# A decoder trunk whose eight experts take their places in another order

## The chip, the cores and the metric

The kernel runs on one core of one Trainium2 chip. The metric is the time of one execution on the device, in microseconds (us). One further execution was taken by the hardware profiler; its rows are what the prediction argues from. Of the core's engines four matter here: TensorE (matmuls; PE in the rows, and PEld for its weight loads), VectorE (DVE), ScalarE (ACT), and SyncE (SP), which computes nothing and issues the loads from memory (DMAs).

## The reference

The model has two layers over 256 tokens of width 1024, all in 32-bit floats. Each layer has a token mixer (attention) and a channel mixer, each followed by a layer norm, and ends with a small gated embedding term. The first layer's channel mixer is dense. The second's is a mixture of eight experts of hidden width 3584, of which every token uses two:

```python
logits = (x @ w_router).astype(jnp.float32)
top_v, top_i = lax.top_k(logits, TOP_K)          # TOP_K = 2 of 8
top_w = jax.nn.softmax(top_v, axis=-1)
gates = jnp.sum(jax.nn.one_hot(top_i, N_EXPERTS) * top_w[..., None], axis=-2)
for e in range(N_EXPERTS):
    out = out + gates[..., e:e + 1] * swiglu(x, w_gate[e], w_up[e], w_down[e])
```

Here `swiglu` is `(silu(x @ w_gate) * (x @ w_up)) @ w_down`. The three matrices of one expert hold 3 x 1024 x 3584 numbers.

## The kernel before

The kernel runs the first layer, the second layer's attention, and then the function `moe`, in which the change lies. There the router picks two experts for every token and counts how many tokens each expert has. The eight experts are then worked through in eight *places*, one after the other. A place doesn't hold a fixed expert: `RANKS` (line 53) says for each place which expert it takes, by its rank in the order of counts. Expert 0 always has rank 0 and the first place; of the others a lower rank has more tokens. The function `order` (lines 721 to 753) turns this into the list `ordi` of expert numbers by place, and SP reads an expert's number from it before the loads of that place (`block_of`, line 973), so that the loads go to that expert's weights.

A place is built for a fixed number of tokens, called slots. Ranks of 5 and above (`SMALL`, line 52) are the three experts with the fewest tokens, and their places have `CS` = 64 slots; the other five have `CM` = 96. Line 925 makes the list:

```python
small = [r >= SMALL for r in RANKS]
groups = [(CS if v else CM) // CG for v in small]
```

Slots are gathered, multiplied and scattered in groups of 32 (`CG`), so a place of 96 slots, called medium here, has three groups and one of 64, called small, has two. A group of 32 token columns is loaded into a quarter of TensorE's array and the weights stream past it (`gate_up_quads` at line 895, `down_quads` at 882 and 885, and the loop at 1141 for the down matmuls of a small place). So a block of weights costs TensorE less in a small place, while the bytes that it takes to load are the same. If an expert has more tokens than slots, extra passes under `tc.If` do the rest; they are outside the order of places.

Within a place the hidden width is cut into four chunks (`CHUNKS`, line 51) of 4, 8, 8 and 8 blocks of 128. The list `seq` (lines 961 to 971) writes the whole work out by hand, block by block: for each chunk the gate-and-up blocks (`w`), then the down blocks (`d`) of the chunk before. Thus the last chunk's down blocks of one place come after the first chunk of the next, and the first chunk of a place is also the end of a stretch that begins in the place before. Gathering the tokens of the next place and scattering the sums of the last one are hung between blocks (`next_expert`, `scatter`). TensorE, VectorE, ScalarE and GpSimd keep this order.

Loads run ahead of the work. `take` issues the loads for as many blocks as the ring of buffers has, and each goes out on SP's queue when its buffer is free, in the order of `seq`. The ring has 21 buffers of 1 MB at first, 20 from the 27th block on, and for the last 26 blocks eight, since the rest are needed by the ending. A block is a gate half and an up half of 512 KB each (issued at line 994), or one down block of 1 MB (line 121). The first chunk of the first place is loaded and multiplied ahead of this list, for all tokens.

After the last place the function `ending` adds the last expert's sums, and does the layer norm and the gated embedding term.

Of the kernel before, what the change touches and what calls it, by code (L numbers as in the profile page):

```python
# [49 lines left out]

CHUNKS = [(0, 4), (4, 8), (12, 8), (20, 8)]
SMALL = 5
RANKS = [0, 5, 1, 2, 6, 3, 7, 4]

# [7 lines left out]
def trunk(ctx: ExitStack, tc: tile.TileContext, a: dict, out: bass.AP):  # L64
# [598 lines left out]
    def route(i, xT, rp, wrh, wrl):  # L663
# [5 lines left out]
        def small(n=NE):  # L669
            at = [next(cells) for _ in range(n // 2)][0]  # L670
            return sm[:, at:at + n]
# [43 lines left out]
        prank = small()  # L715
        for n, r in enumerate(RANKS):
            nc.gpsimd.memset(prank[:, n:n + 1], float(r))
# [54 lines left out]
    def moe(i, x, xT, router, pj):  # L772
        j = i // 2
        with tc.tile_pool(name=f"route{i}", bufs=1, reuse_waits="tile") as rp:
# [49 lines left out]
            def slots(e, p1, small):  # L824

                pe = []
                for t in range(NT):
                    q = rp.tile([P, C], F32, tag=f"pe{t}", bufs=1, name=f"pe{t}")
                    o, v = q, iota1
                    if small:  # L830
                        o = q.rearrange("p (a s) -> p a s", a=2)
                        v = iota1[:, None, :CS].to_broadcast([P, 2, CS])
                    nc.vector.tensor_scalar(o, v, p1[t][:, e:e + 1], None, op0=ALU.is_equal)
                    pe.append(q)
                return pe
# [86 lines left out]
            def main_experts(p1, name, first):  # L922


                small = [r >= SMALL for r in RANKS]
                pe, peT, ob, hT = slots(0, p1, False), None, None, {}
# [627 lines left out]
```

## Time and profile before

| | |
|---|---|
| median of 3 runs | 1344.87 us (1344.11 to 1345.36) |
| the profiled execution | 1344.83 us |
| its span, from the first instruction to the last | 1343.0 us |
| TensorE matmuls, busy | 1311.2 us, 98% of the span |
| bytes read from memory | 433.63 MB |
| mean granted clock of TensorE | 0.995 of full speed |

TensorE counts as busy nearly all the time. Matmuls are pipelined and their ends are modelled, so a share near 100% says that matmuls were in flight and not that the engine was at its peak. The loads of the expert weights share the stretch from about 480 us on with the matmuls that use them.

### The profile page before, as it was taken

What the parts mean: (1) busy time and instruction counts of PE and PEld (TensorE: products, weight loads), DVE (VectorE), ACT (ScalarE), POOL (GpSimd) and SP (SyncE); (2) the same over time, 40 slices, a digit from 0 to 9 for tenths busy, and PEclk for the clock granted to TensorE, in tenths of its full rate; (3) what the DMA queues carried; (4) which work ended last, traced back from release to release, by engine and by line L of the source; (5) the groups of instructions that cost most, each with busy time, mean ns of one, the idle gap of its engine ahead of it and who ended that gap; (6) DMA issues with size and microseconds to landing.
All of it is one profiled execution on the core that took longest, in us unless ns stands there. A gap on an engine that the chain in (4) does not pass through costs nothing.

```text
span 1343.0 us, 29864 instructions
## 1 busy us (share of the span) xinstructions
PE 1311.2 (98%) x12815; PEld 764.9 (57%) x12815; DVE 431.7 (32%) x843; ACT 319.0 (24%) x609; POOL 12.9 (1%) x38
## 2 busy tenths in 40 slices
PE   8999999999999999999999999999999999799987
PEld 6778888888787743453544443363543453343346
DVE  7777444445778611011020011012011011011036
ACT  6865444444458300010000000000000000001013
POOL 1000000000000000000000000000000000000000
PEclk9999999999999999999999999999999999999999
DMA  8439555535358699999999999999999999999970
GB/s 327 156 122 311 190 188 188 188 126 188 119 178 293 262 375 367 402 376 418 414 418 418 415 418 418 415 413 415 414 413 417 409 417 418 408 416 416 415 313 35
DMA packets 141356, 436.71 MB, mean 325 GB/s; under 512 B 11808, under 2 KB 12576, under 8 KB 141216
## 3 DMA queue, kind: packets, MB, share of 16 engines
q1 hardware_dynamic: 141216, 434.72, 83.1%
q8 instruction: 103, 1.69, 0.5%
q14 instruction: 37, 0.30, 0.1%
HBM read 433.63 MB, written 1.05 MB: 324 GB/s over the span
## 4 chain that ended last, share of the span: by engine, by line
PE 82%; DMA 13%; DVE 3%; ACT 1%; issue 1%; POOL 0%; DVEq 0%; SPq 0%; POOLq 0%; ACTq 0%
PE we L895 30%; PE eoe L882 11%; DMA raw_we<-in_w_exp_up_dram 10%; PE eoe L1141 4%; DMA raw_de<-in_w_exp_down_dram 3%; PE gf L159 2%; PE gf L160 2%; PE uf L160 2%; PE uf L159 2%; PE gf L161 2%; PE uf L161 2%; PE fo L159 2%; PE fo L160 2%; PE fo L161 2%; PE pg L936 2%; PE qkv L160 2%
## 5 line engine op out<-in xcount | busy, mean ns | idle before, releaser
L895 PE MATMUL we<-raw_we,xs_e 128*32 128x512 f32 (+1 forms) x5184 | 508.6, 545 | 6.4 <-DMA raw_we<-in_w_exp_up_dram 6.4
L895 PEld LDWEIGHTS we<-raw_we,xs_e 128*32 128x32 f32 x5184 | 166.5, 110 | 318.6 <-issue 280.5
L1033 DVE TENSOR_TENSOR sgh<-we,sgh 128x256 f32<-128x256 f32 (+1 forms) x81 | 32.0, 395 | 590.4 <-ACT sgh L1030 588.8
L882 PE MATMUL eoe<-raw_de,hT 128*32 128x256 f32 x2520 | 186.5, 379 | 0.0
L885 PE MATMUL eoe<-raw_de,hT 128*32 128x256 f32 x840 | 185.3, 379 | 0.0
L1030 ACT ACTIVATE sgh<-we 128x256 f32<-128x256 f32 (+1 forms) x81 | 29.1, 360 | 563.1 <-PE we L895 563.1
L882 PEld LDWEIGHTS eoe<-raw_de,hT 128*32 128x32 f32 x2520 | 103.6, 110 | 77.8 <-issue 5.4
L885 PEld LDWEIGHTS eoe<-raw_de,hT 128*32 128x32 f32 x840 | 92.0, 110 | 0.0
L1141 PE MATMUL eoe<-raw_de,hT 128*32 128x256 f32 x1344 | 77.0, 380 | 4.7 <-DMA raw_de<-in_w_exp_down_dram 4.7
L1141 PEld LDWEIGHTS eoe<-raw_de,hT 128*32 128x32 f32 x1344 | 42.7, 110 | 38.7 <-DMA raw_de<-in_w_exp_down_dram 6.1
L159 PE MATMUL fo<-hi_df,hTh 128*128 128x512 f32 x112 | 43.7, 390 | 0.8 <-ACT hTh L164 0.8
L143 DVE TENSOR_TENSOR lo_gf<-raw_gf,hi_gf 128x1024 fp32r<-128x1024 f32 x28 | 33.2, 1222 | 34.9 <-ACT hi_gf L139 34.9
L143 DVE TENSOR_TENSOR lo_df<-raw_df,hi_df 128x1024 fp32r<-128x1024 f32 x28 | 33.5, 1221 | 33.8 <-ACT hi_df L139 33.8
L159 PE MATMUL gf<-hi_gf,xT_b 128*128 128x512 f32 x112 | 44.2, 394 | 0.0
L161 PE MATMUL gf<-hi_gf,xT_b 128*128 128x512 f32 x112 | 43.7, 390 | 0.0
L161 PE MATMUL uf<-hi_uf,xT_b 128*128 128x512 f32 x112 | 43.7, 390 | 0.0
L159 PE MATMUL uf<-hi_uf,xT_b 128*128 128x512 f32 x112 | 43.7, 390 | 0.0
L160 PE MATMUL gf<-lo_gf,xT_b 128*128 128x512 f32 x112 | 43.6, 389 | 0.0
L160 PE MATMUL fo<-lo_df,hTh 128*128 128x512 f32 x112 | 43.6, 389 | 0.0
L160 PE MATMUL uf<-lo_uf,xT_b 128*128 128x512 f32 x112 | 43.6, 389 | 0.0
L161 PE MATMUL fo<-hi_df,hTl 128*128 128x512 f32 x112 | 43.3, 389 | 0.0
L143 DVE TENSOR_TENSOR lo_uf<-raw_uf,hi_uf 128x1024 fp32r<-128x1024 f32 x28 | 33.1, 1219 | 19.1 <-ACT hi_uf L139 19.1
(292 smaller groups left out, 1596.7 us busy)
## 6 DMA issues: line engine op xcount, KB each, us to landing
raw_de<-in_w_exp_down_dram SPq DMA_DIRECT2D x111, 1024.0 KB, 12.4
raw_we<-in_w_exp_gate_dram SPq DMA_DIRECT2D x220, 512.0 KB, 10.1
raw_we<-in_w_exp_up_dram SPq DMA_DIRECT2D x220, 512.0 KB, 10.0
raw_uf<-in_w_ffn_up_dram SPq DMA_DIRECT2D x14, 1024.0 KB, 5.0
raw_gf<-in_w_ffn_gate_dram SPq DMA_DIRECT2D x14, 1024.0 KB, 5.0
raw_df<-in_w_ffn_down_dram SPq DMA_DIRECT2D x14, 1024.0 KB, 4.7
raw_qkv<-in_w_qkv_dram SPq DMA_DIRECT2D x11, 1024.0 KB, 5.9
raw_wo<-in_w_o_dram SPq DMA_DIRECT2D x8, 1024.0 KB, 5.6
```

What stands on the lines that cost most here:

```text
L143: nc.vector.tensor_tensor(lo[:, cs], raw[:, cs], hi[:, cs].bitcast(F32), op=ALU.subtract)
L159: nc.tensor.matmul(o, xh, wh, start=start, stop=False)
L160: nc.tensor.matmul(o, xh, wl, start=False, stop=False)
L161: nc.tensor.matmul(o, xl, wh, start=False, stop=stop)
L882: nc.tensor.matmul(b[q * CG:(q + 1) * CG, c:c + CQ], xh(q), w[:, k, c0:c0 + CQ], start=start, stop=stop)
L885: nc.tensor.matmul(b[3 * CG:, c:c + CQ], xh(r), w[:, k, c0:c0 + CQ], start=start, stop=stop)
L895: nc.tensor.matmul(b[qs, :2 * nb * CG].rearrange("p (m b r) -> p m b r", m=2, b=nb), xe[:, k, g * CG:(g + 1) * CG], w[..., qs], start=firs ...
L936: nc.tensor.matmul(pg[:, k * n:(k + 1) * n], x[t][:, (h * nk + k) * P:(h * nk + k + 1) * P], pe[t][:, :n], start=t == 0, stop=t == NT - 1)
L1030: nc.scalar.activation(sg[:, g * cols:(g + 1) * cols], b[:, :cols], AF.Silu)
L1033: nc.vector.tensor_tensor(h, b[:, cols:2 * cols], h, op=ALU.mult)
L1141: nc.tensor.matmul(ob[0][q * CG:(q + 1) * CG, r * CQ:(r + 1) * CQ], hT[e, f][:, g, k, :], half[:, k % 2, c * CB + r * CQ:c * CB + (r + 1) ...
```

## The change

One line: the list of ranks by place. The small places, those with a rank of 5, 6 or 7, are the second, third and sixth after the change, and the second, fifth and seventh before it. The medium places come in the same order among themselves, and so do the small ones.

```diff
 CHUNKS = [(0, 4), (4, 8), (12, 8), (20, 8)]
 SMALL = 5
-RANKS = [0, 5, 1, 2, 6, 3, 7, 4]
+RANKS = [0, 5, 6, 1, 2, 7, 3, 4]
```

## Rows read from the trace of the kernel before

**Rows 1.** The page: span, TensorE's busy time, GB/s of loads in forty slices.

```profile
span 1343.0 us, 29864 instructions
PE 1311.2 (98%) x12815; PEld 764.9 (57%) x12815; DVE 431.7 (32%) x843; ACT 319.0 (24%) x609; POOL 12.9 (1%) x38
GB/s 327 156 122 311 190 188 188 188 126 188 119 178 293 262 375 367 402 376 418 414 418 418 415 418 418 415 413 415 414 413 417 409 417 418 408 416 416 415 313 35
```

**Rows 2.** The page's DMA issues: tile, queue, count, size, us to landing.

```profile
raw_de<-in_w_exp_down_dram SPq DMA_DIRECT2D x111, 1024.0 KB, 12.4
raw_we<-in_w_exp_gate_dram SPq DMA_DIRECT2D x220, 512.0 KB, 10.1
```

**Rows 3.** Timeline of TensorE: start, length; second chunk's first matmuls, places 2 to 8.

```profile
595.45 1.90 PE L895 MATMUL we<-raw_we,xs_e 128*32 128x512 f32 x16
...
678.40 3.19 PE L895 MATMUL we<-raw_we,xs_e 128*32 128x512 f32 x28
...
794.03 3.19 PE L895 MATMUL we<-raw_we,xs_e 128*32 128x512 f32 x28
...
905.89 1.47 PE L895 MATMUL we<-raw_we,xs_e 128*32 128x512 f32 x12
...
988.84 2.74 PE L895 MATMUL we<-raw_we,xs_e 128*32 128x512 f32 x22
...
1100.70 3.62 PE L895 MATMUL we<-raw_we,xs_e 128*32 128x512 f32 x32
...
1198.42 1.92 PE L895 MATMUL we<-raw_we,xs_e 128*32 128x512 f32 x16 [0.90 <-DMA raw_we<-in_w_exp_up_dram]
```

**Rows 4.** Timeline of SP: the issue of the same block's gate half, places 3 to 8.

```profile
646.75 0.81 SPq L994 DMA_DIRECT2D raw_we<-in_w_exp_gate_dram  x1
...
754.08 0.34 SPq L994 DMA_DIRECT2D raw_we<-in_w_exp_gate_dram  x1
...
860.96 0.54 SPq L994 DMA_DIRECT2D raw_we<-in_w_exp_gate_dram  x1
...
967.58 0.69 SPq L994 DMA_DIRECT2D raw_we<-in_w_exp_gate_dram  x1
...
1074.97 0.82 SPq L994 DMA_DIRECT2D raw_we<-in_w_exp_gate_dram  x1
...
1181.46 0.40 SPq L994 DMA_DIRECT2D raw_we<-in_w_exp_gate_dram  x1
```

**Rows 5.** Waits of TensorE, 1110 to 1200 us: total, times, longest.

```profile
PE we L895 <- DMA raw_we<-in_w_exp_up_dram: 6.4, 11, 0.9
PE eoe L1141 <- DMA raw_de<-in_w_exp_down_dram: 4.7, 7, 1.5
```

**Rows 6.** Waits of SP, 652 to 1074 us.

```profile
SPq L994 <- DMA raw_de<-in_w_exp_down_dram: 82.1, 45, 3.2
...
SPq L121 <- DMA raw_we<-in_w_exp_up_dram: 17.0, 28, 0.8
SPq L994 <- PE we L895: 7.7, 13, 1.5
...
SPq L994 <- PE eoe L1141: 0.3, 1, 0.3
```

**Rows 7.** Stretches: length, busy time of each engine, clock, DMA share, GB/s.

```profile
652.00:1074.00 422.00, 422.00 (x5355) 188.82 (x5355) 49.07 (x96) 26.09 (x67) 0.00 (x0) 1.00 1.03 415
...
800.00:820.00 20.00, 20.00 (x207) 7.05 (x209) 6.68 (x12) 2.66 (x7) 0.00 (x0) 1.00 1.03 420
...
1140.00:1160.00 20.00, 14.58 (x167) 4.75 (x156) 0.00 (x0) 0.00 (x0) 0.00 (x0) 1.00 1.02 403
...
1300.00:1320.00 20.00, 14.12 (x51) 10.43 (x51) 17.93 (x33) 10.26 (x20) 1.47 (x2) 0.74 0.11 41
```

**Rows 8.** Timelines of SP and TensorE: last expert loads issued, last down matmuls.

```profile
1279.06 0.89 SPq L121 DMA_DIRECT2D raw_de<-in_w_exp_down_dram  x2
...
1299.32 0.39 PE L882 MATMUL eoe<-raw_de,hT 128*32 128x256 f32 x3
```

## The prediction

> **What bounds the kernel now.** I read the page first. It shows TensorE busy for 98% of the span and the loads near 415 GB/s from the nineteenth of its forty slices to the thirty-eighth [rows 1], so it does not say which of the two sets the end. The listing of DMA issues comes next: the expert weights come in 1 MB blocks, either one down block or a gate and an up half of 512 KB [rows 2]. A place takes 28 gate-and-up blocks and 14 down blocks, 42 in all, whether its expert has 96 slots or 64: 44.04 MB. Only TensorE's work depends on the slots.
>
> So I set up two clocks, both read at the same block of every place, the first of its second chunk. From the timeline of TensorE I take when it starts that block, M2 to M8 for places 2 to 8 [rows 3]. From the timeline of SP I take when that block's load is issued, I3 to I8 [rows 4].
>
> - TensorE's steps. M2 to M3 82.95 us (a small place, then a medium one), M3 to M4 115.63 (medium, medium), M4 to M5 111.86 (medium, small), M5 to M6 82.95 (small, medium), M6 to M7 111.86, M7 to M8 97.72. The last is again small to medium, and should have been 82.95: there TensorE stood 14.77 us.
> - The stream's steps. 107.33, 106.88, 106.62, 107.39, 106.49 us; the mean is 106.94 (534.71 / 5), whatever TensorE does.
>
> That is the whole picture: TensorE takes longer than the stream over a medium place (111.86 or 115.63 against 106.94), and about 24 us less over a small one. What it has in hand is M minus I, less the least that this can be. The block at M8 was started the moment its load came (its row names the DMA as releaser), so the least is 1198.42 - 1181.46 = 16.96 us. Spare at M3 to M8 is then 14.7, 23.0, 28.0, 4.3, 8.8 and 0 us. The waits of TensorE stand where this ledger puts them: the view of waits shows it waiting for loads between 1110 and 1200 us, some half a microsecond a block, 6.4 and 4.7 us in its rows [rows 5]. (They sum to less than 14.77; the ends of matmuls in the trace are modelled, so the starts are the safer reading.) From M8 on it works without a wait to the last down matmul at 1299.3 us, and then comes the ending, whose matmuls and vector work are the same in both kernels [rows 8].
>
> **The change, part by part.** Removed and added instructions: none. The two lists hold the same five medium and three small places, so the matmuls, gathers, scatters and loads are the same in number, and so are the bytes. `RANKS` also fills the small table `prank`, with eight one-element writes whatever the numbers are. The register loads on SP that find an expert's weights stay one a place, at the same blocks. What moves is which place is small: 2, 3, 6 in place of 2, 5, 7. I price it by running the ledger again with the same steps.
>
> - Up to the start of place 3 nothing differs.
> - M3. The step is now small to small, which the trace does not have. Replacing the next place by a small one took 115.63 - 111.86 = 3.77 us off a step (the four blocks of the next place's first chunk that lie in it, and its gather), so it is 79.18. Between 79.18 and the 82.95 of the nearest row the end does not change, since a wait follows. Spare at M3: 14.69 - 3.77 = 10.9.
> - M4, small to medium: 82.95 - 106.94 = -24.0. Spare would be -13.1: TensorE waits 13.1 us in place 3 and is at 0.
> - M5, medium to medium: +8.7. M6, medium to small: +4.9, so 13.6.
> - M7, small to medium: -24.0, so -10.4: TensorE waits 10.4 us in place 6 and is at 0.
> - M8, medium to medium: +8.7. TensorE starts the block 16.96 + 8.69 us after its issue: 1181.46 + 25.65 = 1207.11, where it was 1198.42.
>
> The sum is 8.7 us. Waits say the same: 13.1 + 10.4 = 23.5 us against 14.8. In words: before, the last wait lay in place 7 and one medium place was left after it. Now it lies in place 6 and two are left, and over a medium place that follows another TensorE needs 8.7 us more than the stream. The spare time that the loads had gained over places 3 and 4 before (28.0 us at its height) is no longer there to be used up, because small places 2 and 3 in a row empty it at once.
>
> What follows M8 I cost at nothing. Place 8 is the same work, and the loads are further ahead by 8.7 us. For the last loads the ring shrinks to eight blocks, so some of them will be issued up to 8.7 us later, when TensorE has freed the block; the last one went out at 1279.06 and its last matmuls ran at 1299.32, 20 us later [rows 8], and a delay equal to TensorE's own leaves the same 20 us. If that cover were gone, a block late would cost one block's time, 106.94 / 42 = 2.5 us. The ending's own loads wait on the same ring and shift with TensorE.
>
> The unknown is the stream: would it run earlier, now that TensorE frees its blocks sooner? SP waited for TensorE between 652 and 1074 us in nine rows of 7.7 down to 0.3 us, 15.3 us together, and for earlier loads in five rows of 82.1 down to 17.0, 215.8 together [rows 6]. During the former the transfers already issued went on: over that stretch the stream ran at 415 GB/s, and the best slice of 20 us shows 420 [rows 7]. At most 422 x (1 - 415/420) = 5.0 us could come back, at least nothing. I take nothing, since in the stretch where TensorE stood and held no block back, 1140 to 1160 us, the stream made 403 [rows 7], no more than elsewhere. With the 5.0 us the sum would be 3.7 us.
>
> The profiled execution took 1344.83 us, 1.83 us of it around the span, and lies 0.04 us under the median of the runs. 1344.83 + 8.7 = 1353.5 us.
>
> **TensorE's clock.** Between 1140 and 1160 us TensorE was busy for 14.58 of 20 us, with waits for loads between its blocks, and the granted clock stayed at 1.00, the 2.4 GHz level; between 1300 and 1320 us it was busy for about as long, but with 51 matmuls in place of 167, and the clock fell to 0.74 on average, that is to 1.2 GHz for part of the time [rows 7]. The Trainium skill, "TensorE: Matmul & The Clock Gate", section "HAM oscillation — how this bites in real kernels", says that a loop which waits for a load before each short burst of matmuls lets the array fall back to half clock every time. By that rule the 23.5 us of waits would bring half clock into places 3 and 6, and the time would be that of the third rival. By the row it costs nothing; this trace, with the clock at 1.00 through just such waits, does not agree with the rule for waits this short.
>
> **The rivals.** *The wait only moves: no change.* Equal work and equal bytes, so the wait that goes from place 7 comes back in places 3 and 6 and nothing else happens: 1344.8. For it speaks that the stream, at its steady 106.94 us a place, cannot end later. Against it, the end is TensorE's: the two places after the last wait take it 115.63 us and a place's tail, and it is behind the stream for all of it.
>
> *The stream comes earlier: faster.* If the full ring was what held the stream in places 3 to 6, and all 15.3 us of SP's waits on TensorE turned into loading, about 3.8 us would fall in place 3 and 11.5 in places 4 to 6. TensorE would wait 13.1 - 3.8 = 9.3 us in place 3 and not at all in place 6 (-10.4 + 11.5 > 0), 5.5 us less than before: 1339.4. It decides from loads that are 8.7 + 2.7 = 11.4 us early at I7. Against it stands the 5.0 us that the best slice allows. The Trainium skill, "DMA: Bandwidth & Descriptors", section "Where 436 GB/s comes from", has a ceiling of 435.2 GB/s. By it a place's blocks would take 101.2 us, an estimate from that page, and the same ledger gives a single wait of 7.3 us and 1337.3 us; no row here comes above 420.
>
> *The clock falls in the waits: much slower.* In place 6 the wait sets in for the last 10.4 / 24.0 of the place, 46 us of the stream with 36 us of matmuls. At half clock these take 72, so 26 us more: about 1379. The row at 1.00 speaks against it.
>
> **How the numbers follow.** My forecast has 0.85, no change 0.08, the early stream 0.04, the clock (or another slow surprise) 0.03. No change from the kernel before means within 0.2%, 2.7 us, which is about what a measurement of this kernel can tell. Slower 0.88, same 0.08, faster 0.04. The low end of the range is the 5.0 us of the stream, 1348.5. The high end: among the stages the stream's rate differs by a per cent, 1.07 us a place; over the three to four places before M7 that is some 3.5 us, so 1357.
>
> **What would show it.** Right: the step into the third place's marker near 79 us, waits for loads on TensorE in about 700 to 770 and 1030 to 1090 us and none from 1110 to 1200, M8 near 1207, steps of the stream still near 107, granted clock 1.00 in both waits. Wrong: I7 clearly under 1070 (the stream was held by the ring), a step of two medium places other than 115.6, or loads that TensorE waits for after M8.

## The result, and the profile after

The changed kernel took 1353.89 us (median of 4 runs, 1353.33 to 1354.33) where the kernel before took 1344.88. The ratio is 1.0067, 95% interval [1.0055, 1.0079]: 9.0 us slower. The forecast was 1353.5 us, between 1348.5 and 1357.0.

The page of the kernel after, as in [rows 1]. The span is 9.2 us longer, and TensorE's busy time is 1.2 us longer although its instructions are the same in number.

```profile
span 1352.2 us, 29864 instructions
...
PE 1312.4 (97%) x12815; PEld 762.8 (56%) x12815; DVE 431.5 (32%) x843; ACT 318.7 (24%) x609; POOL 12.9 (1%) x38
...
GB/s 329 165 110 309 187 187 187 187 125 187 126 198 277 283 367 372 382 403 416 416 418 419 414 418 419 414 418 407 415 415 415 415 410 418 408 416 388 416 230 34
```

Timeline of TensorE after: the first matmuls of the second chunk of places 2 to 8, M2 to M8, which answer to [rows 3].

```profile
595.10 0.61 PE L895 MATMUL we<-raw_we,xs_e 128*32 128x512 f32 x4
...
674.27 1.04 PE L895 MATMUL we<-raw_we,xs_e 128*32 128x512 f32 x8
...
770.73 0.64 PE L895 MATMUL we<-raw_we,xs_e 128*32 128x512 f32 x4 [0.63 <-DMA raw_we<-in_w_exp_up_dram]
...
886.49 0.61 PE L895 MATMUL we<-raw_we,xs_e 128*32 128x512 f32 x4
...
998.35 0.61 PE L895 MATMUL we<-raw_we,xs_e 128*32 128x512 f32 x4
...
1091.63 0.64 PE L895 MATMUL we<-raw_we,xs_e 128*32 128x512 f32 x4 [0.62 <-DMA raw_we<-in_w_exp_up_dram]
...
1207.29 0.61 PE L895 MATMUL we<-raw_we,xs_e 128*32 128x512 f32 x4
```

Timeline of SP after: the issue of the same blocks' gate halves, I3 to I8, which answer to [rows 4].

```profile
646.85 0.81 SPq L994 DMA_DIRECT2D raw_we<-in_w_exp_gate_dram  x1
...
753.35 0.35 SPq L994 DMA_DIRECT2D raw_we<-in_w_exp_gate_dram  x1
...
861.08 0.35 SPq L994 DMA_DIRECT2D raw_we<-in_w_exp_gate_dram  x1
...
967.68 0.70 SPq L994 DMA_DIRECT2D raw_we<-in_w_exp_gate_dram  x1
...
1074.31 0.74 SPq L994 DMA_DIRECT2D raw_we<-in_w_exp_gate_dram  x1
...
1181.70 0.34 SPq L994 DMA_DIRECT2D raw_we<-in_w_exp_gate_dram  x1
```

The loads go out at the same times as before, within 0.8 us at every marker, and on average 106.97 us a place ((1181.70 - 646.85) / 5). TensorE starts place 3's second chunk 4.1 us earlier than before (674.27 against 678.40), and place 8's 8.9 us later (1207.29 against 1198.42). The wait of TensorE is now in two places: M4 and M7 name the load as what released them, and M8, which did so before, doesn't. The view of waits, between 690 and 770 us and then between 1030 and 1095 us (total, times, longest), against [rows 5]:

```profile
PE we L895 <- DMA raw_we<-in_w_exp_up_dram: 5.0, 9, 0.8
PE eoe L1141 <- DMA raw_de<-in_w_exp_down_dram: 4.2, 8, 0.6
...
PE we L895 <- DMA raw_we<-in_w_exp_up_dram: 5.2, 9, 0.7
PE eoe L1141 <- DMA raw_de<-in_w_exp_down_dram: 2.4, 4, 1.1
```

From 1095 to 1300 us that view is empty. The starts give the full price: M3 to M4 took 96.46 us in place of 82.95, a wait of 13.5, and M6 to M7 93.28, a wait of 10.3. That is 23.8 us against 14.8 before: 9.0 us, the whole loss.

### The profile page after: what moved, and what is told of

Read it like the earlier page. It is cut to its first block, busy times and chain, and to the rows that moved or that the text cites. A ratio compares the mean times of both kernels' runs of the same rounds, so it can differ in the third digit from the quotient of the medians.

```text
span 1352.2 us, 29864 instructions
## 1 busy us (share of the span) xinstructions
PE 1312.4 (97%) x12815; PEld 762.8 (56%) x12815; DVE 431.5 (32%) x843; ACT 318.7 (24%) x609; POOL 12.9 (1%) x38
## 4 chain that ended last, share of the span: by engine, by line
PE 78%; DMA 17%; DVE 3%; ACT 1%; issue 1%; POOL 0%; SPq 0%; DVEq 0%; POOLq 0%; ACTq 0%
PE we L895 27%; PE eoe L882 13%; DMA raw_we<-in_w_exp_up_dram 12%; DMA raw_de<-in_w_exp_down_dram 4%; PE gf L159 2%; PE gf L160 2%; PE gf L161 2%; PE uf L159 2%; PE uf L161 2%; PE uf L160 2%; DMA raw_we<-in_w_exp_gate_dram 2%; PE fo L159 2%; PE fo L160 2%; PE fo L161 2%; PE qkv L161 2%; PE qkv L160 2%
## 5 line engine op out<-in xcount | busy, mean ns | idle before, releaser
L895 PE MATMUL we<-raw_we,xs_e 128*32 128x512 f32 (+1 forms) x5184 | 510.0, 545 | 10.9 <-DMA raw_we<-in_w_exp_up_dram 10.9
L159 PE MATMUL fo<-hi_df,hTh 128*128 128x512 f32 x112 | 43.7, 390 | 0.8 <-ACT hTh L164 0.8
L161 PE MATMUL gf<-hi_gf,xT_b 128*128 128x512 f32 x112 | 43.7, 390 | 0.0
L161 PE MATMUL uf<-hi_uf,xT_b 128*128 128x512 f32 x112 | 43.7, 390 | 0.0
L159 PE MATMUL uf<-hi_uf,xT_b 128*128 128x512 f32 x112 | 43.7, 390 | 0.0
```

Source lines behind the costliest of these rows:

```text
L159: nc.tensor.matmul(o, xh, wh, start=start, stop=False)
L161: nc.tensor.matmul(o, xl, wh, start=False, stop=stop)
L895: nc.tensor.matmul(b[qs, :2 * nb * CG].rearrange("p (m b r) -> p m b r", m=2, b=nb), xe[:, k, g * CG:(g + 1) * CG], w[..., qs], start=firs ...
```

## The experiments

Each of the seven kernels changes the list of places or adds matmuls. The first four compute what the kernel before computes; the last three compute that too, and besides it sums that nobody reads. M and I are the markers of the prediction; a wait is a step of TensorE less the same step without one (82.95 us for small to medium).

**The early half alone, small places 2, 3 and 7.**

```diff
-RANKS = [0, 5, 1, 2, 6, 3, 7, 4]
+RANKS = [0, 5, 6, 1, 2, 3, 7, 4]
```

> Only the early half of the change: the small places are 2, 3 and 7. The ledger: spare 10.9 us at M3, a wait of 13.1 us in place 3, then 0, 8.7, 17.4 and 22.3 us at M4 to M7, and a wait of 1.7 us in place 7, so that M8 is at 1198.4 as in the kernel before: 1344.9 us, up to 1346.5 if the last wait is missed. Rival theory, that two small places in a row are what costs (their wait of 13 us is lost for good): 1353.5 us or more.

1344.51 us against 1344.87, ratio 0.9994, interval [0.9984, 1.0003]: no change that can be measured. Its trace has the wait in place 3 (view of waits from 680 to 780 us), as large as the changed kernel's, and nearly nothing from 1110 to 1300 us; M8 is released by its load, at the time of the kernel before:

```profile
PE we L895 <- DMA raw_we<-in_w_exp_up_dram: 6.2, 11, 0.7
PE eoe L1141 <- DMA raw_de<-in_w_exp_down_dram: 4.1, 8, 0.6
...
PE we L895 <- DMA raw_we<-in_w_exp_up_dram: 0.7, 1, 0.7
PE eoe L1141 <- DMA raw_de<-in_w_exp_down_dram: 0.2, 1, 0.2
...
1198.50 0.64 PE L895 MATMUL we<-raw_we,xs_e 128*32 128x512 f32 x4 [0.70 <-DMA raw_we<-in_w_exp_up_dram]
```

So two small places in a row, and 14.2 us of waiting in the third place (97.15 us from M3 to M4, less 82.95), cost nothing here. The ledger's last wait of 1.7 us was 1.3 (84.28 - 82.95).

**The late half alone, small places 2, 5 and 6.**

```diff
-RANKS = [0, 5, 1, 2, 6, 3, 7, 4]
+RANKS = [0, 5, 1, 2, 6, 7, 3, 4]
```

> Only the late half: the small places are 2, 5 and 6. The ledger: spare 14.7, 23.0, 28.0 and 0.2 us at M3 to M6, one wait of 23.8 us in place 6, and 8.7 us behind at M8: 1353.6 us, with I7 still near 1075. Rival theory, that the wait merely moves with equal work and equal bytes: 1344.9 us. The rival of neighbours also says slower here, so this run alone does not tell it from mine.

1353.63 us, ratio 1.0062, interval [1.0045, 1.0079]: the loss of the whole change. Its waits between 980 and 1095 us, then M7 and M8:

```profile
PE we L895 <- DMA raw_we<-in_w_exp_up_dram: 11.9, 21, 0.7
PE eoe L1141 <- DMA raw_de<-in_w_exp_down_dram: 5.5, 11, 0.6
...
1092.47 0.64 PE L895 MATMUL we<-raw_we,xs_e 128*32 128x512 f32 x4 [0.60 <-DMA raw_we<-in_w_exp_up_dram]
...
1208.14 0.61 PE L895 MATMUL we<-raw_we,xs_e 128*32 128x512 f32 x4
```

The last wait ends at M7 and a step of 115.67 us follows. (M7 and M8 are 0.8 us later than in the changed kernel; the profiled execution took 1354.90 us, 1.3 more than the median, and I7 and I8 are 0.5 and 1.0 us later in it.) That the wait merely moves is ruled out.

**All small places early: 2, 3 and 4.**

```diff
-RANKS = [0, 5, 1, 2, 6, 3, 7, 4]
+RANKS = [0, 5, 6, 7, 1, 2, 3, 4]
```

> All small places early: 2, 3 and 4. The last wait lies in place 4, then come four medium places, so M5 has 0, M6 8.7, M7 17.4 and M8 26.1 us in hand: 1344.9 + 26.1 = 1371.0 us, three times the change's loss. Rival, neighbours: one more pair than the change, near 1362 us. Rival, the stream is held by the ring and comes earlier when TensorE runs close to it: under 1366 us, with I8 at or before 1176.

1370.60 us, ratio 1.0188, interval [1.0171, 1.0205], 25.7 us slower. M5 to M8, then I8:

```profile
877.23 0.64 PE L895 MATMUL we<-raw_we,xs_e 128*32 128x512 f32 x4 [0.60 <-DMA raw_we<-in_w_exp_up_dram]
...
992.88 0.60 PE L895 MATMUL we<-raw_we,xs_e 128*32 128x512 f32 x3
...
1108.53 0.61 PE L895 MATMUL we<-raw_we,xs_e 128*32 128x512 f32 x4
...
1224.18 0.61 PE L895 MATMUL we<-raw_we,xs_e 128*32 128x512 f32 x4
...
1180.88 0.34 SPq L994 DMA_DIRECT2D raw_we<-in_w_exp_gate_dram  x1
```

From M5 on there are three steps of 115.65 us without a wait, and what TensorE has in hand grows by some 8.7 us with each: 0.3, 8.6, 17.2, 26.3 us (M less I less 16.96). The loss is nearly three times that of the change (25.7 and 9.0 us; 26.1 had been forecast). The loads keep their times here too, with I8 0.6 us earlier than before.

**Neighbours late: small places 2, 6 and 7.**

```diff
-RANKS = [0, 5, 1, 2, 6, 3, 7, 4]
+RANKS = [0, 5, 1, 2, 3, 6, 7, 4]
```

> The small places are 2, 6 and 7, again neighbours, but the last wait lies in place 7. The ledger: spare 14.7, 23.0, 31.7, 36.6 and 8.8 us at M3 to M7, a wait of 15.2 us in place 7, M8 as before: 1344.9 us. With 36.6 us in hand TensorE is about 53 us behind the issue, 20 or 21 blocks, as many as the ring has, so the stream may be held a little in place 5: up to 1347. Rival, neighbours: 1353.5 us.

1344.54 us, ratio 0.9997, interval [0.9987, 1.0007]: no change. With the first run this rules the neighbours out. I5 and I6, SP's wait for TensorE between 880 and 990 us (the largest row), and M8:

```profile
860.80 0.53 SPq L994 DMA_DIRECT2D raw_we<-in_w_exp_gate_dram  x1
...
972.20 0.35 SPq L994 DMA_DIRECT2D raw_we<-in_w_exp_gate_dram  x1
...
SPq L994 <- PE we L895: 15.2, 10, 2.0
...
1198.29 0.64 PE L895 MATMUL we<-raw_we,xs_e 128*32 128x512 f32 x4 [0.61 <-DMA raw_we<-in_w_exp_up_dram]
```

Here the ring did hold the stream, as expected: I5 to I6 took 111.40 us in place of 106.9. The next step took 102.95, and by I8 the loads were where they had been. At M6 TensorE had 32.3 us in hand, where the ledger without a ring has 36.6; 32.3 is also what each of the nine traces has at M2, where SP waits for TensorE to free blocks too. What the ring held was mostly the issue and not the transfers: from 860 to 972 us the loads ran at 414 GB/s, and from 972 to 1075 at 409.

**More matmuls in place 3 of the changed kernel.**

```diff
+                        if (m, e, f, h) == ("w", 2, 2, 0):
+                            for v in range(3):
+                                gathered(e, 0, tr_bank)
                         if m == "w":
```

> The changed kernel with more work for TensorE in place 3: at the first block of its third chunk three gathers more, 48 matmuls whose sums nobody reads, 3.7 us each and 11.1 us together by the gather of a small place. They come just ahead of a wait of 13.1 us. Mine: the wait shrinks to about 2 us and the time stays at 1353.9 us. Rival, TensorE's work sets the time everywhere (it is busy for 97% of the span): 1365 us.

1353.84 us, the changed kernel's time. Against the kernel before the ratio is 1.0065, interval [1.0048, 1.0082], where the change alone has 1.0067. Its waits between 652 and 800 us are down from 9.9 us, what the changed kernel has over the same stretch, to 1.8, and M4 still waits for its load:

```profile
PE eoe L1144 <- DMA raw_de<-in_w_exp_down_dram: 1.1, 2, 0.6
PE we L895 <- DMA raw_we<-in_w_exp_up_dram: 0.7, 1, 0.7
...
770.32 0.64 PE L895 MATMUL we<-raw_we,xs_e 128*32 128x512 f32 x4 [0.66 <-DMA raw_we<-in_w_exp_up_dram]
```

**More matmuls in place 7 of the changed kernel.**

```diff
+                        if (m, e, f, h) == ("w", 6, 2, 0):
+                            for v in range(6):
+                                gathered(e, 0, tr_bank)
                         if m == "w":
```

> The changed kernel with more work for TensorE in place 7: at the first block of its third chunk six half gathers more, 48 matmuls whose sums nobody reads, 1.96 us each and 11.8 us together. No wait follows. Mine: all of it is added, 1353.9 + 11.8 = 1365.7 us. Rival, the loads set the time: 1353.9 us.

1365.18 us, 11.3 us above the changed kernel's 1353.89; ratio to the kernel before 1.0150, interval [1.0133, 1.0167]. M7 and M8:

```profile
1090.92 0.64 PE L895 MATMUL we<-raw_we,xs_e 128*32 128x512 f32 x4 [0.61 <-DMA raw_we<-in_w_exp_up_dram]
...
1217.61 0.61 PE L895 MATMUL we<-raw_we,xs_e 128*32 128x512 f32 x4
```

The step is 126.69 us in place of 115.66: the 48 matmuls took 11.0 us, a little less than the 11.8 by which they had been priced, and all of it was added to the time. In place 3 the same number of matmuls, of 64 columns there and 96 here, cost nothing.

**More matmuls in place 7 of the kernel before.** There place 7 is small and has the last wait.

```diff
+                        if (m, e, f, h) == ("w", 6, 2, 0):
+                            for v in range(3):
+                                gathered(e, 0, tr_bank)
                         if m == "w":
```

> The kernel before with more work for TensorE in place 7, small there: at the first block of its third chunk three gathers more whose sums nobody reads, 11.1 us together. It comes ahead of the wait of 14.8 us in that place. Mine: the wait shrinks to about 3.7 us and the time stays at 1344.9 us. Rival, TensorE's work sets the time everywhere: 1356 us.

1345.12 us against 1345.13, ratio 1.0000, interval [0.9990, 1.0009]. The waits from 1105 to 1300 us are 3.3 us in place of 11.1, and M8 is where it was:

```profile
PE eoe L1144 <- DMA raw_de<-in_w_exp_down_dram: 1.7, 4, 0.5
PE we L895 <- DMA raw_we<-in_w_exp_up_dram: 1.6, 3, 0.7
...
1198.67 0.64 PE L895 MATMUL we<-raw_we,xs_e 128*32 128x512 f32 x4 [0.60 <-DMA raw_we<-in_w_exp_up_dram]
```

So it is not the place that makes added work dear, but whether a wait for loads still follows.

## Why the prediction was right

**The ledger.** What TensorE has in hand at each marker, forecast and measured (M less I less 16.96 us):

| marker | forecast | measured |
|---|---|---|
| M3 | 10.9 | 10.5 |
| M4 | 0 | 0.4 |
| M5 | 8.7 | 8.4 |
| M6 | 13.6 | 13.7 |
| M7 | 0 | 0.4 |
| M8 | 8.7 | 8.6 |

The step that the trace before didn't have, small to small, was put at 79.18 us and took 79.17 (674.27 less M2, 595.10). M8 was put at 1207.11 and came at 1207.29. The two waits were put at 13.1 and 10.4 us and took 13.5 and 10.3.

**What follows M8, costed at nothing.** The last down matmuls ran 100.9 us after M8 both times (1308.18 after, 1299.32 in [rows 8]), so no load was missed. The last expert loads did go out 8.9 us later: from 1270 to 1300 us SP waited for TensorE for 20.1 us, and for 8.1 before. They kept their distance from the matmuls. In the rows of SP and TensorE after:

```profile
1287.92 0.89 SPq L121 DMA_DIRECT2D raw_de<-in_w_exp_down_dram  x2
...
1308.18 0.39 PE L882 MATMUL eoe<-raw_de,hT 128*32 128x256 f32 x3
```

The span ends 44.0 us after these matmuls, 43.7 before, and with the 0.2 us at M8 that makes up the half microsecond between the 1351.7 us forecast for the span and 1352.2. On the page, the slice with 388 GB/s near the end (416 in [rows 1]) falls where SP waits for TensorE in this way. The one with 230 (313) doesn't show slower loads: it begins 8.7 us later than before, and in both traces the loads of the ending are in before 1305 us.

**The stream.** I took nothing for an earlier stream, with 5.0 us as the bound. The stretch from 652 to 1074 us after the change made 416 GB/s, where it made 415 [rows 7], although TensorE was idle for 15 us of it. SP's waits for TensorE there are 15.4 us in nine rows, of which the first is shown, as against 15.3 [rows 6]. The two stretches below it are one of 20 us within the first wait of TensorE and one of 60 us around the second.

```profile
SPq L994 <- PE we L895: 7.7, 12, 2.2
...
652.00:1074.00 422.00, 406.86 (x5142) 182.15 (x5145) 46.56 (x92) 25.24 (x64) 0.00 (x0) 1.00 1.03 416
720.00:740.00 20.00, 15.54 (x140) 4.27 (x136) 1.07 (x3) 0.77 (x2) 0.00 (x0) 1.00 1.03 419
1030.00:1090.00 60.00, 53.04 (x748) 26.05 (x744) 4.94 (x12) 3.32 (x9) 0.00 (x0) 1.00 1.03 416
```

So the rival of the earlier stream falls: its condition, loads 11.4 us early at I7, met 0.7 us. (Its 3.8 us for place 3 is a quarter of the 15.3; in the trace before, SP's waits for TensorE from 652 to 762 us sum to 4.6, which changes nothing in this.) The run with places 2, 6 and 7 shows what it looks like when the ring does hold the stream, and there the delay was made up before it mattered.

**The clock.** The same rows have the granted clock at 1.00, the 2.4 GHz level, in both waits, with TensorE busy for 15.54 of 20 us in the first and 53.04 of 60 around the second. In the run with small places 2, 3 and 4, which waited most, it is 1.00 from 700 to 880 us, with TensorE busy for 150.1 of 180. Waits of up to 1.7 us between blocks (the longest, in the run with places 2, 6 and 7) did not show in the mean clock of any profiled execution, 0.995 or 0.996. So the rival of the clock falls for waits this short; what longer ones would do, no run here shows.

**No change.** The rival of equal work and equal bytes fell in the run of the late half. What it overlooks is that the time is the end of the last wait and TensorE's work after it, and that the order decides how much work that is. Two runs with equal sums of work, one with the last small place seventh (1344.5 us) and one with it sixth (1353.6), differ by what a medium place takes TensorE beyond the stream.

**What is not shown.** The eighth place was never small: the ending is written for 96 slots. Nor was an order found that beats the kernel before. Three orders with the last small place seventh agree within their intervals, which fits the ledger: in all three M8 waits for its load, and TensorE's work after it is the same.

## What to carry to other kernels

Where a steady stream of loads feeds stages of unequal work, write down at one marker a stage when the load is issued and when the engine takes it up; the time is then the end of the last wait plus the engine's work after it. Every heavy stage left behind the last wait costs its full excess over the stream, here 8.7 us each, and work ahead of a wait costs nothing as long as it fits into that wait. (Both were shown with the last wait in places 4, 6 and 7, and with some 11 us of work ahead of waits of 13.5 and 14.8 us; more than a wait holds was not tried.) An engine's busy share doesn't show this: added matmuls cost all of their time or none of it in a kernel where TensorE is busy for 97 to 98%.

## What the runs showed of the hardware

TensorE's steps over a place without a wait were the same in every kernel: 82.95 us for small to medium in four of the traces, 79.16 or 79.17 for small to small, 115.63 to 115.76 for medium to medium. Only the waits varied. The stream's step from I3 on wandered more, 106.4 to 107.9 us, except in the run with places 2, 6 and 7, where the ring held the issue (111.40 us, then 102.95). The granted clock was 1.00 from 652 to 1300 us in all nine traces.
